# A down projection that takes the gate and up projections' form: two slices of an FFN on one core

## The chip, the cores and the metric

The kernel runs on one core of a Trainium2 chip. The metric is device time in microseconds (us) of that core for one launch. Five engines work side by side, each with its own queue of instructions: PE (matmuls; PEld is the same engine's weight load), DVE (elementwise work), ACT (copies and functions), POOL, and SP, which here mostly issues DMA loads. A matmul holds one operand in the array (the stationary one, 128x128) and streams the other past it; its sums go to PSUM, eight banks of 128 x 512 f32 words. All data are float32. The reference is computed to nearly full float32 precision by splitting each operand into a high part (`hi`, rounded to the type that a PE takes in one pass, F32R) and the remainder (`lo`), and by adding three products: hi*hi, hi*lo and lo*hi.

## The reference

One encoder layer for two request groups that share weights: 256 positions of a new stream and 64 of a running one, together T = 320 columns. The parts ahead of the FFN are left out here; the change touches only the FFN (D = 2048, D_FF = 5632).

```python
h = x + merged @ w_out[l]
hn = rmsnorm(h, norm_ffn[l])
gu = hn @ w_gate_up[l]
h = h + (jax.nn.silu(gu[..., :D_FF]) * gu[..., D_FF:]) @ w_down[l]
...
return rmsnorm(x, norm_final), ...
```

## The kernel before

Activations lie with features on the 128 partitions and the 320 positions on the free axis, so a projection's output block m (128 features x 320 positions) is a sum over the k blocks of its input. D is 16 blocks, D_FF is 44. The FFN runs in three slices of 16, 16 and 12 blocks of D_FF (`SLICES`). For each slice the kernel makes the gate and up projections of these blocks, four blocks at a time, then the down projection of the slice into all 16 blocks of the residual stream `hs`.

There are two forms of a projection:

- **Narrow** (`block`, `product`, lines 84 to 100, and the loop over `lead`, lines 687 to 695). The weight is the stationary operand. For each weight block 128x128 there are three matmuls over 320 columns: high weight with high activation (L87), high weight with low activation (L88), low weight with high activation (L89). `weights` (L75) loads 128x1024 f32 (512 KB) by SP's queue; `halved` (L67) makes the high part on ACT (L70) and the low part on DVE (L71). The result leaves PSUM with one addition on DVE (`down_out`, L671). At the start of a slice's down projection six outputs are built together (`lead`), first from the slice's first eight blocks, so that the last blocks of `act` have time to be finished.
- **Wide** (`quad`, lines 543 to 578). Four output blocks at once, called a quad here. For each k the high weight is now the streamed operand, 512 columns wide (four output blocks of 128), and the activation is stationary, in five pieces: two 128-column pieces of its high part, the two matching pieces of its low part, and one piece that holds the 64 last positions of both. That is the main part of a quad: 16 k x 5 = 80 matmuls (L562) into three PSUM banks, with eight loads of 512 KB (L546), each covering two k. The low weights follow in the narrow form: 4 outputs x 16 k = 64 matmuls of 320 columns (L572), each output's sum copied to `total` by DVE (L573). The main part comes out with positions on partitions, so it has to be turned: `quad_turn` copies the three banks to `flat` as two planes of 16-bit halves on ACT (L587) and issues one DMA transpose per plane from ACT's queue (L588). `quad_join` merges the turned planes on DVE (L594, two copies), adds them to `total` (L596, L597), and `gate_out` (rms factor L601, Silu on ACT L602) or `up_out` (L606, L607, split into hi and lo L610, L611) finishes four blocks. `lows` holds the eight low weight tiles of a quad until the low sums use them: four buffers of tag `wl` and five of tag `low`, nine in turn (`count[0] % 9`). Raw weights have three buffers, high weights four.

What sets the order: every engine takes its instructions in the order of its queue, and that order is the scheduler's, from the order in which the code issues them. `tick()` counts steps (one for each loaded tile, one for each low sum), and `at(tick, fn)` puts work that is due later behind such a step: the join is issued five steps after the main part's end, the two halves of gate_out or up_out at six and seven. PSUM has three banks `acc`, four `aux` and one `aux1`. Gate quads build in `acc`, up quads in `aux`; the low sums take `aux1` and `aux` by turns.

A tile of `act` is hi and lo, 320 columns each. The same pool ("D", 24 buffers) holds the 16 `act` pairs of one slice and the 8 pairs of `hs`.

Of the kernel before, what the change touches and what calls it, by code (L numbers as in the profile page):

```python
# [34 lines left out]
def stream_step(ctx: ExitStack, tc: tile.TileContext, xT, w_in, w_a, w_b, w_out, w_gu, w_down,  # L35
# [501 lines left out]

    fctx = ExitStack()
    fpool = fctx.enter_context(tc.tile_pool(name="ffn", bufs=1))
    count = [0]  # L540

    def quad(b0, main, done):
        lows = []
        for c in range(0, KD, 2):
            raw = wraw.tile([P, HALF * P], F32, tag="raw", name="raw")
            nc.sync.dma_start(out=raw.rearrange("p (b k) -> p b k", b=4),  # L546
                              in_=w_gu[b0 : b0 + 4, :, c * P : (c + 2) * P].rearrange("b p k -> p b k"))
# [6 lines left out]
            nc.scalar.copy(out=wh, in_=raw)  # L554
            nc.vector.tensor_tensor(out=wl, in0=raw, in1=wh.bitcast(F32), op=ALU.subtract)  # L555
            wh = wh.rearrange("p (b k) -> p b k", b=4)
            lows.append(wl)
            for j in range(2):
                k = c + j
                w, x = wh[:, :, j * P : (j + 1) * P], hg[k][2]  # L560
                for i, at0 in enumerate((0, T + TS, P, T + TS + P, TP)):
                    nc.tensor.matmul(main[i // 2].rearrange("p (b m) -> p b m", b=4), x[:, at0 : at0 + P], w,  # L562
                                     start=k == 0 and i % 2 == 0, stop=k == KD - 1 and (i % 2 == 1 or i == 4))
            tick()
        total = fpool.tile([P, 4, T], F32, tag="sum", bufs=2, name="sum")
        now = state["tick"]
        turning = quad_turn(main)
        for b in range(4):
            ps = aux1() if b % 2 == 0 else aux()
            for k in range(KD):  # L570
                at0 = (2 * b + k % 2) * P
                nc.tensor.matmul(ps[:, :T], lows[k // 2][:, at0 : at0 + P], hg[k][0], start=k == 0, stop=k == KD - 1)  # L572
            nc.vector.tensor_copy(total[:, b, :], ps[:, :T])  # L573
            tick()
        at(now + 5, quad_join, total, *turning)
        for i in range(2):
            at(now + 6 + i, done, total, 2 * i)
        return total

    def quad_turn(main):  # L580
# [7 lines left out]
            nc.scalar.dma_start_transpose(out=turned[:, i], in_=planes[:, i, :])  # L588
        return flat, turned

    def quad_join(total, flat, turned):
        rows = flat.bitcast(U16).rearrange("p (b c t w) -> p b c t w", b=4, c=3, w=2)
        for i in range(2):
            nc.vector.tensor_copy(rows[:, :, :, :, 1 - i], turned[:, i].rearrange("p (c b) t -> p b c t", c=3))  # L594
# [9 lines left out]
    def up_out(gate, total, b):  # L604
        t = total[:, b : b + 2, :]
        nc.vector.tensor_tensor(out=t, in0=t, in1=got["rh"][:, None, :].to_broadcast([P, 2, T]), op=ALU.mult)  # L606
        nc.vector.tensor_tensor(out=t, in0=t, in1=gate[:, b : b + 2, :], op=ALU.mult)  # L607
        for j in range(2):
            a = pair("act", dt=F32R)
            nc.scalar.copy(out=a[:, 0, :], in_=t[:, j, :])  # L610
            nc.vector.tensor_tensor(out=a[:, 1, :], in0=t[:, j, :], in1=a[:, 0, :].bitcast(F32), op=ALU.subtract)  # L611
            act.append(a)

    def gain(m, half):
        r = CUTS[half]
# [53 lines left out]

    def down_out(m, ps):  # L670
        nc.vector.tensor_tensor(out=hs[m], in0=ps[:, :T], in1=hs[m], op=ALU.add)  # L671
        if s0 + n < KF:
            return
# [5 lines left out]
        nc.vector.tensor_scalar(out=hs[m], in0=hs[m], scalar1=g_fin[:, m : m + 1], scalar2=None, op0=ALU.mult)  # L679

    for s0, n in SLICES:
        act = []
        for b0 in range(s0, s0 + n, 4):
            gate = quad(b0, [acc() for _ in range(3)], gate_out)
            quad(KF + b0, [aux() for _ in range(3)], lambda total, b, gate=gate: up_out(gate, total, b))
        final = s0 + n == KF
        lead = [acc() for _ in range(3)] + [aux() for _ in range(3)]
        for k0, k1 in ((0, HALF), (HALF, n)):
            for m, ps in enumerate(lead):
                w = weights(w_down[m][:, (s0 + k0) * P : (s0 + k1) * P], k1 - k0)  # L690
                for k in range(k0, k1):
                    product(ps, w, k - k0, (act[k][:, 0, :], act[k][:, 1, :]), k == 0, k == n - 1)
                if k1 == n:
                    down_out(m, ps)
                tick()
        halves = [(t[:, 0, :], t[:, 1, :]) for t in act]
        for m in range(len(lead), KD - LATE if final else KD):
            down_out(m, block(w_down[m][:, s0 * P : (s0 + n) * P], halves))
    fctx.close()
    kept = pool("kept")  # L700
    for m in range(KD - LATE, KD):
# [144 lines left out]
```

## Time and profile before

| | us |
|---|---|
| median of 3 runs | 1693.46 (1691.39 to 1704.93) |
| profiled execution, its own time | 1698.68 |
| its span, first to last instruction | 1696.9 |
| PE busy | 1682.7 |
| DVE busy | 971.8 |
| ACT busy | 734.1 |

The FFN in that execution, by the first matmul of each part:

| part | from | us |
|---|---|---|
| gate and up, slice of 16 (8 quads) | 760.88 | 220.32 |
| down, narrow, 16 x 16 blocks | 981.20 | 112.64 |
| gate and up, slice of 16 (8 quads) | 1093.84 | 224.51 |
| down, narrow, 16 x 16 blocks | 1318.35 | 113.30 |
| gate and up, slice of 12 (6 quads) | 1431.65 | 165.25 |
| down of the last slice, and the end | 1596.90 | 100.00 |

The profiled execution took 1698.68 us, of which 1.8 us lie around the span; it is 5.2 us above the median of the runs shown. Matmuls overlap, so PE counts as busy through almost everything; what a stretch costs is read from the start of its first matmul to the start of the next stretch's first. Equal work in two rows of the second table (the two slices of 16) that takes unequal time shows where PE waited.

### The profile page before, as it was taken

To read this page: it belongs to the slowest core of one execution; us is meant where nothing else is said; L and a number is where in the kernel's file an instruction comes from. 1 tells how busy PE (TensorE), PEld (TensorE's weight loads), DVE (VectorE), ACT (ScalarE), POOL (GpSimd) and SP (SyncE) were. 2 spreads that over 40 slices of the span, in tenths; PEclk is the share of its full clock that TensorE was granted. 3 is DMA by queue.
4 is the path that set the end of the run, shared out by engine and by line. 5 is a ranking of instruction groups with operands and counts; after the bars stand their busy time and mean duration, and the time that the engine had idled before them with its cause. 6 is when DMAs were issued, how large, how long until landed. Compare 5 with 4: busy or idle time off the path is not lost.

```text
span 1696.9 us, 25604 instructions
## 1 busy us (share of the span) xinstructions
PE 1682.7 (99%) x10496; PEld 1607.0 (95%) x10496; DVE 971.8 (57%) x1261; ACT 734.1 (43%) x956; POOL 38.9 (2%) x68
## 2 busy tenths in 40 slices
PE   9999999999999999999999999999999999999998
PEld 9999999999999999998988899988888999889898
DVE  7665656544444445556666664446666644475666
ACT  7555645433333333444444532343445323444343
POOL 1100001000000000000000000000000000000000
PEclk9999999999999999999999999999999999999999
DMA  7866555444444444556656655566666545566554
GB/s 280 258 178 177 160 163 164 118 152 151 151 149 149 150 149 162 173 167 178 175 173 182 193 167 150 156 166 170 180 167 189 166 150 162 164 189 174 149 156 124
DMA packets 236982, 285.49 MB, mean 168 GB/s; under 512 B 98081, under 2 KB 194337, under 8 KB 236865
## 3 DMA queue, kind: packets, MB, share of 16 engines
q1 hardware_dynamic: 164016, 257.72, 48.6%
q10 hardware_dynamic: 70224, 17.88, 6.0%
q0 software_dynamic: 2624, 8.26, 1.6%
q8 instruction: 82, 1.34, 0.3%
q14 instruction: 36, 0.29, 0.1%
HBM read 256.03 MB, written 5.51 MB: 154 GB/s over the span
## 4 chain that ended last, share of the span: by engine, by line
PE 87%; DMA 5%; DVE 4%; ACT 2%; issue 1%; ACTq 0%; SPq 0%; DVEq 0%
PE acc L89 18%; PE acc L87 18%; PE acc L88 18%; PE acc L562 9%; PE aux L572 8%; PE aux L562 7%; DMA raw<-w_gu 2%; DMA turned<-flat 2%; PE aux L89 2%; PE aux L88 2%; PE aux L87 2%; ACT flat L587 1%; DVE low L555 1%; DVE flat L594 1%; PE acc L639 1%
## 5 line engine op out<-in xcount | busy, mean ns | idle before, releaser
L70 ACT CAST wh<-raw 128x1024 fp32r<-128x1024 f32 (+2 forms) x296 | 302.7, 1023 | 561.1 <-PE acc L88 382.4
L71 DVE TENSOR_TENSOR wl<-raw,wh 128x1024 fp32r<-128x1024 f32 (+2 forms) x296 | 351.7, 1191 | 224.4 <-ACT wh L70 223.3
L87 PE MATMUL acc<-A,wh 128*128 128x320 f32 x1088 | 337.7, 311 | 0.4 <-ACT A L108 0.4
L88 PE MATMUL acc<-A,wh 128*128 128x320 f32 x1088 | 336.5, 309 | 0.0
L89 PE MATMUL acc<-A,wl 128*128 128x320 f32 x1088 | 336.3, 309 | 0.0
L554 ACT CAST wh<-raw 128x1024 fp32r<-128x1024 f32 x176 | 185.3, 1054 | 317.8 <-DMA raw<-w_gu 259.9
L87 PEld LDWEIGHTS acc<-A,wh 128*128 128x128 f32 x1088 | 204.4, 188 | 2.3 <-issue 1.5
L88 PEld LDWEIGHTS acc<-A,wh 128*128 128x128 f32 x1088 | 204.5, 188 | 0.3 <-DVE A L110 0.3
L89 PEld LDWEIGHTS acc<-A,wl 128*128 128x128 f32 x1088 | 204.3, 188 | 0.2 <-DVE wl L71 0.2
L562 PE MATMUL acc<-wh,A 128*128 128x512 f32 x880 | 203.2, 390 | 1.1 <-ACT wh L554 1.0
L562 PE MATMUL aux<-wh,A 128*128 128x512 f32 x880 | 201.5, 389 | 0.0
L562 PEld LDWEIGHTS acc<-wh,A 128*128 128x128 f32 x880 | 164.2, 188 | 37.0 <-ACT wh L554 3.5
L562 PEld LDWEIGHTS aux<-wh,A 128*128 128x128 f32 x880 | 164.8, 188 | 33.7
L89 PE MATMUL acc<-act,wl 128*128 128x320 f32 x500 | 155.1, 311 | 2.8 <-DVE wl L71 2.8
L87 PE MATMUL acc<-act,wh 128*128 128x320 f32 x500 | 155.0, 310 | 0.0
L88 PE MATMUL acc<-act,wh 128*128 128x320 f32 x500 | 154.9, 310 | 0.0
L555 DVE TENSOR_TENSOR low<-raw,wh 128x1024 fp32r<-128x1024 f32 x96 | 117.8, 1235 | 37.4 <-ACT wh L554 37.1
L573 DVE COPY sum<-aux 128x320 f32<-128x320 f32 x88 | 43.0, 489 | 157.8 <-PE aux L572 157.8
L572 PE MATMUL aux<-A,low 128*128 128x320 f32 x768 | 128.6, 309 | 0.1
L572 PEld LDWEIGHTS aux<-A,low 128*128 128x128 f32 x768 | 117.1, 188 | 1.4 <-ACT flat L587 0.4
L555 DVE TENSOR_TENSOR wl<-raw,wh 128x1024 fp32r<-128x1024 f32 x80 | 97.6, 1224 | 22.1 <-ACT wh L554 22.1
L572 PE MATMUL aux<-A,wl 128*128 128x320 f32 x640 | 109.0, 309 | 0.8 <-ACT flat L587 0.8
(221 smaller groups left out, 2297.5 us busy)
## 6 DMA issues: line engine op xcount, KB each, us to landing
raw<-w_gu SPq DMA_DIRECT2D x176, 512.0 KB, 3.8
raw<-w_in SPq DMA_DIRECT2D x141, 512.0 KB, 3.7
raw<-w_down SPq DMA_DIRECT2D x80, 512.0 KB, 3.7
raw<-w_out SPq DMA_DIRECT2D x32, 512.0 KB, 3.6
raw<-w_a SPq DMA_DIRECT2D x16, 512.0 KB, 3.4
raw<-w_b SPq DMA_DIRECT2D x16, 512.0 KB, 3.5
raw<-w_down SPq DMA_DIRECT2D x16, 256.0 KB, 2.8
xr<-xT POOLq DMA_DIRECT2D x16, 160.0 KB, 2.6
```

Source lines behind the costliest of these rows:

```text
L70: nc.scalar.copy(out=wh[:, : n * P], in_=raw[:, : n * P])
L71: nc.vector.tensor_tensor(out=wl[:, : n * P], in0=raw[:, : n * P], in1=wh[:, : n * P].bitcast(F32), op=ALU.subtract)
L87: nc.tensor.matmul(ps[:, :T], a, x[0], start=first, stop=False)
L88: nc.tensor.matmul(ps[:, :T], a, x[1], start=False, stop=False)
L89: nc.tensor.matmul(ps[:, :T], b, x[0], start=False, stop=last)
L554: nc.scalar.copy(out=wh, in_=raw)
L555: nc.vector.tensor_tensor(out=wl, in0=raw, in1=wh.bitcast(F32), op=ALU.subtract)
L562: nc.tensor.matmul(main[i // 2].rearrange("p (b m) -> p b m", b=4), x[:, at0 : at0 + P], w, start=k == 0 and i % 2 == 0, stop=k == KD - 1 ...
L572: nc.tensor.matmul(ps[:, :T], lows[k // 2][:, at0 : at0 + P], hg[k][0], start=k == 0, stop=k == KD - 1)
L573: nc.vector.tensor_copy(total[:, b, :], ps[:, :T])
L587: tc.keep_in_program_order(nc.scalar.copy(out=planes[:, i, c * 512 : (c + 1) * 512], in_=hw[:, :, 1 - i]))
L594: nc.vector.tensor_copy(rows[:, :, :, :, 1 - i], turned[:, i].rearrange("p (c b) t -> p b c t", c=3))
```

## The change

Four things change, all in the FFN.

1. `quad` takes any source of weights and any list of stationary activations. The down projections of the first two slices (not the last) are made as four quads each, with the slice's 16 `act` blocks as the stationary operands and `w_down` as the streamed one. The result is added to `hs` by `add_down`, four blocks per quad in two additions of 128x640. For this, `up_out` stores the low part of `act` in the piecewise order that the wide form needs (`apart`): two subtractions, 64 and 256 columns, for one of 320.
2. Between a slice's last up quad and its down quads, the first gate quad of the next slice is run; its result waits in a tile of its own (`held`) until the down quads are done.
3. `quad_join` is placed behind the copy of the last low sum (`tc.issue_after(copied.ins)`), and its step and those of the finishing work are each one later (6, 7 and 8).
4. The low weights' ring has eight buffers, four `wl` and four `low`, for nine; PSUM sets `acc` and `aux` alternate by a count of quads.

The last slice's down projection stays narrow, with `lead` outside the loop.

```diff
-    def quad(b0, main, done):
+    def quad(src, xs, done, tag="sum"):
         lows = []
-        for c in range(0, KD, 2):
+        nk = len(xs)
+        main = [(acc, aux)[count[1] % 2]() for _ in range(3)]
+        count[1] += 1
+        for c in range(0, nk, 2):
...
-            if count[0] % 9 < 4:
+            if count[0] % 8 < 4:
                 wl = wsplit.tile([P, HALF * P], F32R, tag="wl", name="wl")
             else:
-                wl = fpool.tile([P, HALF * P], F32R, tag="low", bufs=5, name="low")
+                wl = fpool.tile([P, HALF * P], F32R, tag="low", bufs=4, name="low")
...
-            nc.vector.tensor_copy(total[:, b, :], ps[:, :T])
+            copied = nc.vector.tensor_copy(total[:, b, :], ps[:, :T])
             tick()
-        at(now + 5, quad_join, total, *turning)
+        at(now + 6, quad_join, copied.ins, total, *turning)
         for i in range(2):
-            at(now + 6 + i, done, total, 2 * i)
+            at(now + 7 + i, done, total, 2 * i)
         return total
...
-    def quad_join(total, flat, turned):
+    def quad_join(behind, total, flat, turned):
+        with tc.issue_after(behind):
+            join(total, flat, turned)
...
+            for r0, r1, at0 in (((TP, T, T), (0, TP, T + TS)) if apart else ((0, T, T),)):
+                nc.vector.tensor_tensor(out=flat[:, at0 : at0 + r1 - r0], in0=t[:, j, r0:r1],
+                                        in1=a[:, 0, r0:r1].bitcast(F32), op=ALU.subtract)
+            to.append(a)
+
+    def add_down(m0, total, b):
+        y = ypair[(m0 + b) // 2]
+        nc.vector.tensor_tensor(out=y, in0=total[:, b : b + 2, :], in1=y, op=ALU.add)
...
+        for b0 in range(s0, s0 + n, 4):
+            gate = gate_quad(b0) if held is None else held
+            held = None
+            up_quad(b0, gate, act, not final)
+        if not final:
+            held = gate_quad(s0 + n, "held")
+            wide_act = [t.rearrange("p i t -> p (i t)") for t in act]
+            for m in range(0, KD, 4):
+                quad(w_down[m : m + 4, :, s0 * P : (s0 + n) * P], wide_act, lambda total, b, m=m: add_down(m, total, b))
```

How the instructions stand now, at three places. First PE at the end of the first slice's up quads. Before, the last low sums (L572) are followed by the narrow triples of the down projection, 768 matmuls of 320 columns:

```order
L572 MATMUL aux<-A,wl 128x320 x4
L572 MATMUL aux<-A,low 128x320 x10
L572 MATMUL aux<-A,wl 128x320 x2
L87 MATMUL acc<-act,wh 128x320
L88 MATMUL acc<-act,wh 128x320
L89 MATMUL acc<-act,wl 128x320
L87 MATMUL acc<-act,wh 128x320
L88 MATMUL acc<-act,wh 128x320
```

Now, at the same place (`acc<-wh,A` is the held gate quad, `<-wh,act` and `<-act,wl` or `low` the first down quad, and L565 and L575 are what L562 and L572 were):

```order
L575 MATMUL aux<-A,low 128x320 x8
L565 MATMUL acc<-wh,A 128x512 x80
L575 MATMUL aux_9671<-A,wl 128x320 x8
L575 MATMUL aux_9671<-A,low 128x320 x8
L575 MATMUL aux<-A,wl 128x320 x8
L575 MATMUL aux<-A,low 128x320 x8
L575 MATMUL aux_9707<-A,wl 128x320 x8
L575 MATMUL aux_9707<-A,low 128x320 x8
L575 MATMUL aux<-A,wl 128x320 x8
L575 MATMUL aux<-A,low 128x320 x8
L565 MATMUL aux<-wh,act 128x512 x80
L575 MATMUL aux_9893<-act,wl 128x320 x8
```

What moved: a gate quad stands between the last up quad and the down projection, and each four outputs of the down projection are 80 matmuls of 512 columns and 64 of 320, where they were 192 of 320.

Second, DVE around the join of an up quad (the first of the FFN). L573 copies the low sums, L594 merges the turned planes, L555 makes low weights, of this quad's last tiles (`x4`) and then of the next quad's. Before:

```order
L555 TENSOR_TENSOR low<-raw,wh 128x1024 x4
L573 COPY sum<-aux_8053 128x320
L573 COPY sum<-aux 128x320
L573 COPY sum<-aux_8089 128x320
L555 TENSOR_TENSOR low<-raw,wh 128x1024
L594 COPY flat<-turned 128x1536
L573 COPY sum<-aux 128x320
L594 COPY flat<-turned 128x1536
L555 TENSOR_TENSOR wl<-raw,wh 128x1024
```

Now (L576, L601 and L558 are the same instructions):

```order
L558 TENSOR_TENSOR low<-raw,wh 128x1024 x3
L576 COPY sum<-aux_8053 128x320
L576 COPY sum<-aux 128x320
L576 COPY sum<-aux_8089 128x320
L558 TENSOR_TENSOR wl<-raw,wh 128x1024 x2
L576 COPY sum<-aux 128x320
L601 COPY flat<-turned 128x1536 x2
L558 TENSOR_TENSOR wl<-raw,wh 128x1024
```

What moved: the last low sum's copy now stands ahead of the first merging copy, and one more of the next quad's low weights is made between the third and the fourth low sum (it was the last of the `x4` before). In both, two low weights of the next quad stand ahead of the join and the third behind it.

Third, DVE at the end of the last up quad, where the last slice's narrow down projection begins (L71 makes that projection's low weights). Before, both merging copies stand ahead of its first low weight:

```order
L573 COPY sum<-aux 128x320
L594 COPY flat<-turned 128x1536
L573 COPY sum<-aux_14633 128x320
L594 COPY flat<-turned 128x1536
L71 TENSOR_TENSOR wl<-raw,wh 128x1024
L573 COPY sum<-aux 128x320
L71 TENSOR_TENSOR wl<-raw,wh 128x1024
```

Now two of these low weights stand ahead of the join:

```order
L576 COPY sum<-aux 128x320
L576 COPY sum<-aux_14441 128x320
L71 TENSOR_TENSOR wl<-raw,wh 128x1024 x2
L576 COPY sum<-aux 128x320
L601 COPY flat<-turned 128x1536 x2
L71 TENSOR_TENSOR wl<-raw,wh 128x1024
```

What moved: the join, from ahead of the third low sum's copy to behind the fourth's, and with it the first two low weights of the down projection, which no longer stand behind it.

More of the change, by code (lines that the diff above doesn't have):

```diff
@@ L559, in quad @@
                 k = c + j
[L560 removed]
+                w, x = wh[:, :, j * P : (j + 1) * P], xs[k]
                 for i, at0 in enumerate((0, T + TS, P, T + TS + P, TP)):
                     nc.tensor.matmul(main[i // 2].rearrange("p (b m) -> p b m", b=4), x[:, at0 : at0 + P], w,
[L563 removed]
+                                     start=k == 0 and i % 2 == 0, stop=k == nk - 1 and (i % 2 == 1 or i == 4))
             tick()
[L565 removed]
+        total = fpool.tile([P, 4, T], F32, tag=tag, bufs=2 if tag == "sum" else 1, name=tag)
         now = state["tick"]
@@ L589, in quad_turn, with join @@
         return flat, turned
-    def quad_join(total, flat, turned):
+    def quad_join(behind, total, flat, turned):
+        with tc.issue_after(behind):
+            join(total, flat, turned)
+    def join(total, flat, turned):
         rows = flat.bitcast(U16).rearrange("p (b c t w) -> p b c t w", b=4, c=3, w=2)
@@ L602, in gate_out, with up_out @@
         nc.scalar.activation(out=t, in_=t, func=AF.Silu)
-    def up_out(gate, total, b):
+    def up_out(to, apart, gate, total, b):
         t = total[:, b : b + 2, :]
@@ L671, in down_out @@
         nc.vector.tensor_tensor(out=hs[m], in0=ps[:, :T], in1=hs[m], op=ALU.add)
-        if s0 + n < KF:
-            return
         if m == 0:
@@ L679, in down_out, with gate_quad, up_quad @@
         nc.vector.tensor_scalar(out=hs[m], in0=hs[m], scalar1=g_fin[:, m : m + 1], scalar2=None, op0=ALU.mult)
+    wide_x = [t[2] for t in hg]
+    def gate_quad(b0, tag="sum"):
+        return quad(w_gu[b0 : b0 + 4], wide_x, gate_out, tag)
+    def up_quad(b0, gate, to, apart):
+        quad(w_gu[KF + b0 : KF + b0 + 4], wide_x, lambda total, b: up_out(to, apart, gate, total, b))
+    held = None
     for s0, n in SLICES:
         act = []
+        final = s0 + n == KF
         for b0 in range(s0, s0 + n, 4):
-            gate = quad(b0, [acc() for _ in range(3)], gate_out)
@@ L685, in stream_step @@
[L685 to L695, printed above, removed]
@@ L696, in stream_step @@
-        halves = [(t[:, 0, :], t[:, 1, :]) for t in act]
-        for m in range(len(lead), KD - LATE if final else KD):
-            down_out(m, block(w_down[m][:, s0 * P : (s0 + n) * P], halves))
+            gate = gate_quad(b0) if held is None else held
+            held = None
+            up_quad(b0, gate, act, not final)
[4 more added lines that the diff above has]
+                quad(w_down[m : m + 4, :, s0 * P : (s0 + n) * P], wide_act, lambda total, b, m=m: add_down(m, total, b))
@@ new lines, in stream_step @@
+    lead = [acc() for _ in range(3)] + [aux() for _ in range(3)]
+    for k0, k1 in ((0, HALF), (HALF, n)):
+        for m, ps in enumerate(lead):
+            w = weights(w_down[m][:, (s0 + k0) * P : (s0 + k1) * P], k1 - k0)
+            for k in range(k0, k1):
+                product(ps, w, k - k0, (act[k][:, 0, :], act[k][:, 1, :]), k == 0, k == n - 1)
+            if k1 == n:
+                down_out(m, ps)
+            tick()
+    halves = [(t[:, 0, :], t[:, 1, :]) for t in act]
+    for m in range(len(lead), KD - LATE):
+        down_out(m, block(w_down[m][:, s0 * P : (s0 + n) * P], halves))
```

11 lines of the change are left out of this document (5 added, 6 removed).

## The prediction

> **What bounds the kernel now.** I read the page first, then the stretches of the FFN, then PE in order of time at each place where a stretch is longer than its matmuls, and then the engine that PE waited for there.
>
> ```profile
> span 1696.9 us, 25604 instructions
> PE 1682.7 (99%) x10496; PEld 1607.0 (95%) x10496; DVE 971.8 (57%) x1261; ACT 734.1 (43%) x956; POOL 38.9 (2%) x68
> PE 87%; DMA 5%; DVE 4%; ACT 2%; issue 1%; ACTq 0%; SPq 0%; DVEq 0%
> ```
>
> PE is busy 99% of the span and carries 87% of the chain that ended last; DVE and ACT have room. So the change is worth what it takes off PE: a shorter stream of matmuls, and fewer gaps in it. The stretches of the FFN (columns: window, length, busy time of PE, PEld, DVE, ACT, POOL, clock, DMA share, GB/s):
>
> ```profile
> 760.88:981.20 220.32, 220.32 (x1155) 195.20 (x1154) 137.05 (x162) 105.27 (x138) 2.15 (x1) 1.00 0.65 179
> 981.20:1093.84 112.64, 112.64 (x771) 112.64 (x770) 55.99 (x61) 33.95 (x35) 0.00 (x0) 1.00 0.51 155
> 1093.84:1318.35 224.51, 222.50 (x1155) 194.72 (x1153) 133.74 (x155) 101.78 (x133) 0.00 (x0) 1.00 0.64 174
> 1318.35:1431.65 113.30, 112.89 (x770) 112.63 (x769) 55.84 (x61) 33.95 (x35) 0.00 (x0) 1.00 0.51 157
> 1431.65:1596.90 165.25, 165.25 (x866) 146.41 (x865) 95.06 (x111) 75.00 (x98) 0.00 (x0) 1.00 0.62 175
> ```
>
> The first down projection is 768 narrow matmuls in 112.64 us: 146.7 ns each. The first slice's eight quads take 220.32, 27.54 each, and the last slice's six 165.25, again 27.54: no gap. The second slice lost 224.51 - 220.32 = 4.19 us in its quads and 113.30 - 112.64 = 0.66 in its down projection. One quad on PE:
>
> ```profile
> 1139.57 1.33 PE L572 MATMUL aux<-A,wl 128*128 128x320 f32 x8
> 1148.95 18.32 PE L562 MATMUL acc<-wh,A 128*128 128x512 f32 x80
> 1167.11 0.45 PE L572 MATMUL aux<-A,low 128*128 128x320 f32 x2
> ```
>
> From 1148.95 to 1167.11 are 18.16 us for 80 matmuls of 512 columns, 227.0 ns each; the low sums ahead of them took 9.38, that is 64 at 146.6.
>
> **Part 1, the down projection of two slices in the wide form.** For four outputs, 192 narrow matmuls are replaced by 80 + 64: 28.16 us by 27.54. A slice of 16 has four such quads, 110.16 for 112.64, and two slices save 2 x 2.48 = 4.96 us. The columns streamed are the same (61,440 per four outputs in both forms); what is saved is the cost of 48 matmuls that no longer exist. A stretch of w_down with act as the stationary operand isn't in this trace. The nearest row is the gate quad's, of the same shape, 227.0 ns. The other end is the narrow row's price per column, 146.7 x 512 / 320 = 234.7 ns, at which nothing is saved. I take 227.0, since 1,760 such matmuls ran at it.
>
> The Trainium skill, "TensorE: Matmul & The Clock Gate", Back-to-back issue gap, has a matmul at N / 2.4 + 2.5 ns, so 215.8 and 135.8 here. The rows show 227.0 and 146.7, about 13.5 ns over the streaming and not 2.5, and the measurement decides; by the page's figures I estimate a saving of 0.96 us where the rows give 4.96.
>
> What the quads add off PE, from these groups:
>
> ```profile
> L587 ACT COPY flat<-acc 128x512 uint16<-128x512 uint16 x66 | 34.3, 592 | 7.6 <-ACT wh L554 6.6 <-PE acc L562 1.1
> L588 ACTq DMA_TRANSPOSE turned<-flat x44: 1430/1450/1692, 780.1 to 1593.1; - x44
> L594 DVE COPY flat<-turned 128x1536 uint16<-128x1536 uint16 x44 | 45.3, 1051 | 40.6 <-DMA turned<-flat 40.6
> L606 DVE TENSOR_TENSOR sum<-sum,rh 128x640 f32<-128x640 f32 x22 | 17.1, 822 | 0.0
> raw<-w_gu SPq DMA_DIRECT2D x176, 512.0 KB, 3.8
> raw<-w_down SPq DMA_DIRECT2D x80, 512.0 KB, 3.7
> ```
>
> ACT gets six plane copies and two transposes per quad, 6 x 0.59 + 2 x 1.45 = 6.5 us, 26 per slice beside the 33.95 it was busy. DVE gets two merges of 1.05 and, at L606's price, two additions into hs of 0.82, besides sums and copies that quads of gate and up have too; those quads keep DVE busy 137.05 / 8 = 17 us and ACT 13 of 27.54. That is the cover, about 10 us each per quad; if it were gone PE would show gaps in all quads of the first slice, and it shows none. The split of act's low part makes 32 more DVE instructions, at most 0.5 us each, in quads with that same cover (0.49 is the 128x320 copy's price in part 3; these are 64 and 256 wide). SP issues as many loads (64 of 512 KB); cut as w_gu's they land in 3.8 us for 3.7. Nothing new is on POOL.
>
> **Part 2, the held gate quad.** It only changes places: its eight loads are ahead of the down projection's 32 on SP's queue, and act now has 27.54 us of PE work to be finished under. I cost it at nothing: finishing a quad is part of DVE's 17 us per quad, so it ends inside the next one. The second slice's 0.66 us (narrow triples waiting for a low weight behind a late join) goes with the narrow form.
>
> **Part 3, the join behind the fourth low sum.** A quiet quad (DVE, then ACT's casts for the next quad's last loads):
>
> ```profile
> 1147.22 1.22 DVE L555 TENSOR_TENSOR wl<-raw,wh 128x1024 fp32r<-128x1024 f32 x1
> 1150.21 1.06 DVE L594 COPY flat<-turned 128x1536 uint16<-128x1536 uint16 x1 [1.78 <-DMA turned<-flat]
> 1151.14 0.49 DVE L573 COPY sum<-aux 128x320 f32<-128x320 f32 x1
> 1152.47 1.23 DVE L555 TENSOR_TENSOR wl<-raw,wh 128x1024 fp32r<-128x1024 f32 x1
> 1162.38 1.05 ACT L554 CAST wh<-raw 128x1024 fp32r<-128x1024 f32 x1
> ```
>
> What stands behind the join on DVE is the next quad's third low weight; only then is a raw buffer free, SP loads, ACT casts, PE streams. The join began 1150.21 - 1139.57 = 10.64 us after the low sums did; the last cast ended at 1163.43 and PE needed it after 70 matmuls, 1148.95 + 70 x 0.227 = 1164.84. The slack is 1.4 us. In a late quad:
>
> ```profile
> 1208.43 1.07 DVE L594 COPY flat<-turned 128x1536 uint16<-128x1536 uint16 x1 [4.58 <-DMA turned<-flat]
> 1204.42 11.52 PE L562 MATMUL acc<-wh,A 128*128 128x512 f32 x50
> 1216.55 2.59 PE L562 MATMUL acc<-wh,A 128*128 128x512 f32 x10 [0.61 <-ACT wh L554]
> 1224.34 0.89 PE L572 MATMUL aux<-A,low 128*128 128x320 f32 x5
> 1194.65 0.74 PE L572 MATMUL aux<-A,low 128*128 128x320 f32 x4
> 1315.90 0.56 PE L572 MATMUL aux<-A,wl 128*128 128x320 f32 x2 [0.75 <-ACT flat L587]
> ```
>
> Here it began 13.78 us after, 3.14 later; less the slack, 1.74 us should be lost, and 1224.34 - 1204.42 - 18.16 = 1.76 were. So a quad loses what its join begins after about 12.0. Now two low weights (from 7.65 after the low sums' start, 1.13 apart) and the copy stand ahead: the join can begin at about 10.4 and has no copy between its halves, so it may begin as late as 12.4. The last row is another quad of that slice, where PE itself waited for a PSUM bank that ACT's plane copies had not emptied. Copies and transposes were late where they stood behind casts that waited for loads; with eight buffers the fourth load of the next quad starts at about 8.9 and no longer beside the transposes. So I expect the 4.19 us to be gone. Both ends: all kept (0 gained), or lateness in more quads (a rival below).
>
> **Part 4, the end of the last up quad.**
>
> ```profile
> 1596.83 1.05 DVE L594 COPY flat<-turned 128x1536 uint16<-128x1536 uint16 x1 [3.93 <-DMA turned<-flat]
> 1599.07 1.21 DVE L71 TENSOR_TENSOR wl<-raw,wh 128x1024 fp32r<-128x1024 f32 x1
> 1597.63 0.31 PE L88 MATMUL acc<-act,wh 128*128 128x320 f32 x1
> 1600.33 0.64 PE L89 MATMUL acc<-act,wl 128*128 128x320 f32 x1 [2.39 <-DVE wl L71]
> 1603.52 0.31 PE L89 MATMUL acc<-act,wl 128*128 128x320 f32 x1
> 1600.33:1603.40 3.07, 3.07 (x12) 3.07 (x13) 3.07 (x4) 0.00 (x0) 0.00 (x0) 0.52 0.61 172
> ```
>
> The first low weight of the last down projection stood behind the join; PE stopped, and after the gap the granted clock was 0.52 for 3.07 us. From 1597.63 to 1603.52 are 5.89 us for 13 matmuls worth 1.91: 3.98 us lost. Now two low weights stand ahead of the join, enough for 48 matmuls, 7.0 us, and the first needs no more than 7.65 + 1.2 of the 9.38 us of low sums. The 3.98 us go. Next late is the third, due 16.4 us after the low sums' start and done at about 13.8.
>
> **The sum**, against the profiled execution: 1698.68 - 4.96 - 0.66 - 4.19 - 3.98 = 1684.9. That execution stands 5.2 us above the median of 1693.46, about as much as the second slice's 4.85, which I take for late transposes of that one execution. By the median, without those terms: 1693.46 - 4.96 - 3.98 = 1684.5. Both agree; if the runs of the median have the second slice's gaps as well, 1693.46 - 13.79 = 1679.7.
>
> **The rivals.**
>
> Only the stream is saved: the gaps come back elsewhere (another late low weight at the last slice, other late transposes). 1693.46 - 4.96 = 1688.5. For it: each gap has its own cause in a queue's order, and all orders changed. Against: the new order names no late step.
>
> The fixed cost per matmul is not saved in the new stretch, because act's tiles stream no better than the narrow form: 227.0 becomes up to 234.7, and the forecast becomes 1684.9 + 4.0 to 5.0, about 1689. The page's rule above would give this too. Against: the same shape ran at 227.0 throughout.
>
> Slower: the ring of eight. With the spare buffer gone, the next quad's first low weight can't be made until the fourth low sum has read its tile. If this moves loads so that they run beside the transposes, and the joins of all 30 quads begin later than 12.4 us after the low sums' start, each loses the excess. The forecast's 9 us are eaten at 0.3 us per quad (join at 12.7), and 1% is lost at 0.85 (13.3, while the late quad above had 13.78): at that quad's 13.78, 30 x 1.4 = 42, so 1726. For it: several quads of one slice were late like this. Against: the two low weights that stand ahead of the join are the same in number as before.
>
> **How the numbers follow.** The forecast holds 0.72, its own range 1679 to 1690; only the stream 0.14; no saving per matmul 0.04; the ring of eight 0.10, half of it within 1%. About 1%, 17 us, is what a measurement of this kernel can tell from no change (the three runs lie 13.5 apart). Nothing in the sum reaches 1676.5: faster by over 1% 0.02; slower 0.05; within 1% 0.93. The range goes from 1678 (all gaps in the median, a little more) to 1696 (only the stream, and the mild half of the ring).
>
> **What would show it.** Right: each of the two down stretches takes 110.2 us from first 512-wide matmul to the next up quad's; 30 quads of 27.54; no PE gap at the last down projection and a clock of 1.00 there; DVE's first merge of a quad begins 10.4 to 12 us after the low sums. Wrong: PE gaps ended by ACT's casts at a quad's sixth to eighth load, main parts over 18.16, or matmuls over 227 ns.

## The result and the profile after

| | median us | runs |
|---|---|---|
| before | 1694.11 | 20, 1691.27 to 1714.24 |
| after | 1710.47 | 20, 1699.85 to 1719.59 |

The ratio is 1.0079, 95% interval 1.0055 to 1.0103: slower by 0.8%, 25.6 us above the forecast of 1684.9 and outside its range. Medians and ratios, here and below, leave out a run marked as slow (over 1.5% above the fastest of the same kernel); that is one of e9's four. The profiled execution took 1711.4 us, with a span of 1709.6. From the page of the changed kernel, the span, the engines, and the chain of work that ended last:

```profile
span 1709.6 us, 24995 instructions
PE 1684.1 (99%) x10112; PEld 1575.8 (92%) x10112; DVE 1008.9 (59%) x1341; ACT 759.7 (44%) x1004; POOL 38.9 (2%) x68
PE 75%; DMA 11%; DVE 6%; ACT 4%; issue 2%; ACTq 1%; SPq 0%; DVEq 0%
```

The busy share of PE says nothing here: it is 99% in both kernels. What moved is the chain: PE carries 75% of it for 87%, DMA 11% for 5%, DVE and ACT 10% for 6%. The stretches, with the columns of the prediction's (nine quads, four down quads, eight quads, four down quads, five quads, the end):

```profile
760.57:1010.47 249.90, 248.75 (x1299) 219.36 (x1297) 156.31 (x202) 117.53 (x155) 2.15 (x1) 1.00 0.65 176
1010.47:1122.76 112.29, 110.80 (x578) 97.45 (x577) 65.08 (x73) 47.09 (x58) 0.00 (x0) 1.00 0.62 175
1122.76:1353.46 230.70, 224.15 (x1154) 194.26 (x1153) 143.19 (x185) 101.06 (x134) 0.00 (x0) 1.00 0.65 175
1353.46:1467.21 113.75, 111.87 (x579) 97.14 (x578) 65.23 (x73) 47.10 (x58) 0.00 (x0) 1.00 0.62 173
1467.21:1613.61 146.40, 141.07 (x722) 123.85 (x721) 86.93 (x103) 62.77 (x82) 0.00 (x0) 0.98 0.63 172
1613.61:1709.62 96.01, 88.10 (x602) 87.52 (x600) 67.27 (x135) 39.19 (x71) 0.00 (x0) 0.98 0.49 145
```

At 27.54 us a quad the first five rows should be 247.86, 110.16, 220.32, 110.16 and 137.70. They are 2.04, 2.13, 10.38, 3.59 and 8.70 longer: 26.84 us lost in the 30 quads. The end took 96.01 where it took 100.00. The account closes: 1684.9 + 26.84 = 1711.7, for the 1711.4 measured. So the other terms of the sum came out, and the quads, whose 4.19 us of gaps were to go, lost 26.84 instead.

**The worst quad.** Its low sums began at 1457.82. First ACT, from the last cast ahead of the plane copies, then DVE, then PE in the next quad's main part:

```profile
1461.38 1.05 ACT L557 CAST wh<-raw 128x1024 fp32r<-128x1024 f32 x1 [1.64 <-DMA raw<-w_gu]
1462.33 1.55 ACT L590 COPY flat<-acc 128x512 uint16<-128x512 uint16 x3
1463.91 1.46 ACTq L591 DMA_TRANSPOSE turned<-flat  x1
1465.41 1.56 ACT L590 COPY flat<-acc 128x512 uint16<-128x512 uint16 x3 [1.53 <-issue]
1467.01 1.64 ACTq L591 DMA_TRANSPOSE turned<-flat  x1
...
1465.47 2.35 DVE L558 TENSOR_TENSOR wl<-raw,wh 128x1024 fp32r<-128x1024 f32 x2
1467.74 0.48 DVE L576 COPY sum<-aux 128x320 f32<-128x320 f32 x1
1476.43 1.97 DVE L601 COPY flat<-turned 128x1536 uint16<-128x1536 uint16 x2 [8.21 <-DMA turned<-flat]
1478.28 1.21 DVE L558 TENSOR_TENSOR wl<-raw,wh 128x1024 fp32r<-128x1024 f32 x1
...
1467.21 9.25 PE L565 MATMUL aux<-wh,A 128*128 128x512 f32 x40
1477.34 2.56 PE L565 MATMUL aux<-wh,A 128*128 128x512 f32 x10 [0.88 <-ACT wh L557]
1484.35 9.89 PE L565 MATMUL aux<-wh,A 128*128 128x512 f32 x30 [4.45 <-ACT wh L557]
```

Read it from the top. The plane copies waited on ACT behind a cast that waited for a load of the next quad. So the second transpose was issued 9.2 us after the low sums' start, and the join, ready on DVE at 1468.2, waited 8.21 us for it. The third low weight stood behind the join, with it the load that its raw buffer lets go, and PE ran out of high weights twice. This main part took 26.86 us for 18.16. In the second gap PE stood for 4.45 us, and the granted clock behind it was 0.50:

```profile
1484.35:1490.20 5.85, 5.85 (x14) 4.59 (x15) 3.92 (x4) 2.10 (x2) 0.00 (x0) 0.50 0.81 244
```

What the transpose met, by the DMA view of 1462 to 1478 (tile, issues, KB, median us from issue to landing; the 6.3 is the median of 3.7 and 8.95):

```profile
raw<-w_gu SPq DMA_DIRECT2D x2, 512.0 KB, 6.2
turned<-flat ACTq DMA_TRANSPOSE x2, 6.3
```

The two low weights that stand ahead of the join let two raw buffers go. Their loads were issued at 1466.7 and 1467.8 and landed after 4.17 and 8.30 us; the second transpose, issued between them, took 8.95. Over all transposes, before and then after:

```profile
DMA to landing us min/median/max: 3.6/3.7/6.1
...
DMA to landing us min/median/max: 3.6/3.8/9.0
```

Sorted by its own issue, the second transpose of a quad in the changed kernel landed after 3.83 us on the mean where it was issued less than 7.5 us after the low sums' start (21 quads), and after 6.19 us where later (9 quads, 7.8 to 9.6 us). Those nine are the nine whose join began later than 12.4 us.

### The profile page after: what moved, and what is told of

The parts are those of the page before. It is cut to its first block, busy times and chain, and to the rows that moved or that the text cites. A ratio compares the mean times of both kernels' runs of the same rounds, so it can differ in the third digit from the quotient of the medians.

```text
span 1709.6 us, 24995 instructions
## 1 busy us (share of the span) xinstructions
PE 1684.1 (99%) x10112; PEld 1575.8 (92%) x10112; DVE 1008.9 (59%) x1341; ACT 759.7 (44%) x1004; POOL 38.9 (2%) x68
## 4 chain that ended last, share of the span: by engine, by line
PE 75%; DMA 11%; DVE 6%; ACT 4%; issue 2%; ACTq 1%; SPq 0%; DVEq 0%
PE acc L87 14%; PE acc L88 14%; PE acc L89 14%; PE aux L575 9%; PE acc L565 9%; PE aux L565 8%; DMA turned<-flat 4%; DMA raw<-w_down 4%; DMA raw<-w_gu 3%; ACT flat L590 2%; DVE low L558 2%; ACT wh L557 2%; DVE flat L601 2%; ACTq L591 1%; DVE sum L603 1%
## 5 line engine op out<-in xcount | busy, mean ns | idle before, releaser
L557 ACT CAST wh<-raw 128x1024 fp32r<-128x1024 f32 x240 | 252.6, 1053 | 436.3 <-DMA raw<-w_gu 282.2
L70 ACT CAST wh<-raw 128x1024 fp32r<-128x1024 f32 (+2 forms) x232 | 235.7, 1016 | 406.0 <-PE acc L88 290.8
L71 DVE TENSOR_TENSOR wl<-raw,wh 128x1024 fp32r<-128x1024 f32 (+2 forms) x232 | 273.4, 1182 | 164.4 <-ACT wh L70 164.2
L565 PE MATMUL aux<-wh,A 128*128 128x512 f32 x880 | 205.8, 394 | 7.0 <-ACT wh L557 7.0
L565 PE MATMUL acc<-wh,A 128*128 128x512 f32 x880 | 204.8, 391 | 3.8 <-ACT wh L557 3.7
L565 PEld LDWEIGHTS aux<-wh,A 128*128 128x128 f32 x880 | 166.4, 190 | 43.4 <-ACT wh L557 9.1
L565 PEld LDWEIGHTS acc<-wh,A 128*128 128x128 f32 x880 | 163.8, 188 | 41.7 <-ACT wh L557 8.6
L576 DVE COPY sum<-aux 128x320 f32<-128x320 f32 x112 | 54.8, 489 | 234.9 <-PE aux L575 234.9
L558 DVE TENSOR_TENSOR low<-raw,wh 128x1024 fp32r<-128x1024 f32 x120 | 147.2, 1234 | 40.1 <-ACT wh L557 39.9
L558 DVE TENSOR_TENSOR wl<-raw,wh 128x1024 fp32r<-128x1024 f32 x120 | 143.9, 1219 | 7.1 <-PE aux L575 3.7
L575 PE MATMUL aux<-A,wl 128*128 128x320 f32 x704 | 117.6, 309 | 2.2 <-ACT flat L590 2.2
L575 PE MATMUL aux<-A,low 128*128 128x320 f32 x704 | 117.5, 309 | 0.0
L575 PEld LDWEIGHTS aux<-A,wl 128*128 128x128 f32 x704 | 107.6, 188 | 4.4 <-ACT flat L590 2.7
L575 PEld LDWEIGHTS aux<-A,low 128*128 128x128 f32 x704 | 106.9, 188 | 0.0
L601 DVE COPY flat<-turned 128x1536 uint16<-128x1536 uint16 x60 | 59.4, 1045 | 42.5 <-DMA turned<-flat 40.8
L87 PE MATMUL acc<-mh,wh 128*128 128x320 f32 x256 | 79.1, 309 | 0.0
```

The source lines that it names most:

```text
L70: nc.scalar.copy(out=wh[:, : n * P], in_=raw[:, : n * P])
L71: nc.vector.tensor_tensor(out=wl[:, : n * P], in0=raw[:, : n * P], in1=wh[:, : n * P].bitcast(F32), op=ALU.subtract)
L87: nc.tensor.matmul(ps[:, :T], a, x[0], start=first, stop=False)
L576: copied = nc.vector.tensor_copy(total[:, b, :], ps[:, :T])
```

## The experiments

Two questions: what makes the transposes late, and what makes a late one slow. A quad's turn is its plane copies and its two transposes. "Ring" is the number of low weight buffers. Lost in the quads is, as above, the time over 27.54 per quad in the profiled execution; transposes and joins are counted from the start of their quad's low sums.

**e1: the changed kernel with nine buffers.** Room for the ninth comes from two kinds of scratch tile (`bb` and `xr`) that share another's place.

```diff
-        refine(r, ms, t320("bb"))
+        refine(r, ms, t320("mg", 1))
...
-        x = t320("xr")
+        x = t320(f"gate{m % 2}", 1)
...
-            if count[0] % 8 < 4:
+            if count[0] % 9 < 4:
...
-                wl = fpool.tile([P, HALF * P], F32R, tag="low", bufs=4, name="low")
+                wl = fpool.tile([P, HALF * P], F32R, tag="low", bufs=5, name="low")
```

> The changed kernel with nine low-weight buffers again (room for the ninth is made by sharing three scratch tiles ahead of the FFN). Theory RING (the lost spare buffer makes two loads of every quad start together at 8.9 and 10.0 us after the low sums' start, where they fall on the second transpose): the loss of about 27 us in the 30 quads mostly goes, 1685 to 1692 us, ratio to the kernel before 0.995 to 0.999. Theory TURN (the transposes are issued late because plane copies stand on ACT behind casts that wait for loads): little changes, 1700 to 1711, since the casts stand where they did. Theory JOIN (the join's new place): 1705 to 1711.

1685.78 us (7 runs, 1685.37 to 1686.80), ratio to before 0.9892 (0.9855 to 0.9928). The page's chain and three stretches, the four first down quads, the four later ones, and all 30 quads:

```profile
PE 99%; DVE 0%; DMA 0%; SPq 0%; ACT 0%; issue 0%; DVEq 0%
...
1008.52:1118.68 110.16, 110.16 (x578) 97.60 (x577) 64.75 (x73) 46.99 (x58) 0.00 (x0) 1.00 0.66 182
1339.00:1449.16 110.16, 110.16 (x578) 97.60 (x577) 64.65 (x73) 46.76 (x58) 0.00 (x0) 1.00 0.66 182
...
760.65:1586.86 826.21, 826.21 (x4322) 731.98 (x4321) 514.51 (x632) 373.75 (x487) 2.15 (x1) 1.00 0.66 180
```

The last row is 30 x 27.54 = 826.2: nothing is lost. The quad that was the worst above, here with its low sums from 1439.78:

```profile
1439.58 1.05 ACT L557 CAST wh<-raw 128x1024 fp32r<-128x1024 f32 x1 [1.43 <-DMA raw<-w_gu]
1440.54 1.54 ACT L590 COPY flat<-acc 128x512 uint16<-128x512 uint16 x3
1442.03 1.05 ACT L557 CAST wh<-raw 128x1024 fp32r<-128x1024 f32 x1
1442.11 1.47 ACTq L591 DMA_TRANSPOSE turned<-flat  x1
1443.62 1.56 ACT L590 COPY flat<-acc 128x512 uint16<-128x512 uint16 x3 [0.54 <-ACT wh L557]
1445.21 1.45 ACTq L591 DMA_TRANSPOSE turned<-flat  x1
...
1450.39 1.97 DVE L601 COPY flat<-turned 128x1536 uint16<-128x1536 uint16 x2
```

The same cast ended 0.85 us after the low sums' start, not 4.6, the second transpose was issued at 5.4, and the join found its data there at 10.6. This is what the ninth buffer does. With it, one low weight of the next quad can be made before the low sums begin, so a raw buffer is free, and the loads and casts of the next quad come a step earlier. With eight, that low weight has to wait until the low sums release a tile, some 7.6 us after they begin, and ACT's casts wait for loads just when the plane copies are due behind them.

e1's time fits its theory RING, but the mechanism named there does not hold: with nine buffers, too, two loads start at 8.9 and 10.0 us in every quad (the next quad's fifth and sixth, where with eight they are the fourth and fifth). What differs is the transposes: in e1 the second transpose of each quad was issued at 4.2 to 6.0 us, and no join began after 10.9. That is TURN's mechanism, and TURN's own time for e1 (1700 to 1711) was a miss, since the casts did not stand where they did.

**e3: eight buffers, but the plane copies don't wait.** The casts of the next quad's first three tiles are placed behind the second transpose on ACT.

```diff
+    last = [None]
...
-            nc.scalar.copy(out=wh, in_=raw)
+            if last[0] is None or c > 4:
+                nc.scalar.copy(out=wh, in_=raw)
+            else:
+                with tc.issue_after(last[0]):
+                    nc.scalar.copy(out=wh, in_=raw)
...
+            sent = nc.scalar.dma_start_transpose(out=turned[:, i], in_=planes[:, i, :])
+        last[0] = sent.ins
```

> The changed kernel with the first three casts of a quad placed on ACT's queue behind the previous quad's second transpose, so that plane copies wait for PE alone. TURN: second transposes are issued about 4.3 us after the low sums' start in every quad, land before 8.9 in about 3.7 us each, joins begin at 10.3, quads take 27.54, and the time is 1683 to 1688, ratio 0.994 to 0.997. RING alone: the two loads still start at 8.9 and 10.0, so if these hurt by themselves (late for PE, not by meeting a transpose) the loss stays, over 1700. JOIN: the loss stays, 1705 to 1711.

1685.86 us (9 runs, 1685.01 to 1687.45), ratio 0.9924 (0.9896 to 0.9952); 0.04 us lost in the quads, as TURN expected. ACT in the quad that was the worst, and all 30 quads:

```profile
1440.21 1.56 ACT L595 COPY flat<-acc 128x512 uint16<-128x512 uint16 x3 [3.62 <-PE acc L570]
...
1444.90 1.45 ACTq L596 DMA_TRANSPOSE turned<-flat  x1
...
761.53:1587.77 826.24, 826.24 (x4322) 732.00 (x4321) 515.28 (x632) 373.28 (x487) 2.15 (x1) 1.00 0.66 180
```

The plane copies now wait for PE alone. The second transpose goes out at 4.2 to 5.1 us in every quad but the last (6.8), and the two loads still start at 8.9 and 10.0. So with the join at its new place eight buffers cost nothing by themselves: they cost what the casts ahead of the plane copies wait. The shared scratch tiles aren't what e1 gained by: e3 has none of them, and e9 below has them and is slow.

**e4: the kernel before with e3's edit.**

> The kernel before with the same edit. TURN: its second slice's gaps, where a run has them, go; the gap at the last down projection shrinks or stays, since the join still stands ahead of that low weight: 1687 to 1693, ratio 0.996 to 1.000. RING and JOIN: no change, 1692 to 1697.

1702.80 us (10 runs, 1700.82 to 1703.70), ratio 1.0027 (1.0001 to 1.0053): a miss. The quads still lost 5.72, and the end got worse. DVE and PE at the last down projection:

```profile
1601.49 1.02 DVE L600 COPY flat<-turned 128x1536 uint16<-128x1536 uint16 x1 [4.39 <-DMA turned<-flat]
1602.40 1.22 DVE L71 TENSOR_TENSOR wl<-raw,wh 128x1024 fp32r<-128x1024 f32 x1
...
1603.67 0.41 PE L89 MATMUL acc<-act,wl 128*128 128x320 f32 x1 [3.56 <-DVE wl L71]
```

The edit covers the casts in `quad`, not those of `weights` (L70), which stand ahead of the last quad's plane copies; and the join at its old place still has the narrow projection's first low weight behind it. Of the second transposes only those of each slice's last quad were issued after 7.5 us (8.3 to 9.7). The gap at the last down projection was 3.56 us, for 2.39 before. An early turn doesn't replace the join's new place.

**e6: the kernel before with the join's new place alone** (nine buffers, narrow down projection).

```diff
-        at(now + 5, quad_join, total, *turning)
+        at(now + 6, behind, copied.ins, total, *turning)
...
+    def behind(ins, total, flat, turned):
+        with tc.issue_after(ins):
+            quad_join(total, flat, turned)
```

> The kernel before (narrow down projections, nine low-weight buffers) with only the join placed behind the fourth low sum's copy and its steps one later. Theory TERMS (the sum of the prediction holds where no transpose is late): the 3.98 us gap at the last down projection goes, and the second slice's gaps with it or not: 1687 to 1691, ratio 0.996 to 0.998. Theory JOIN (the join's new place costs time by itself): 1695 or more.

1690.24 us (10 runs, 1689.90 to 1690.99), ratio 0.9952 (0.9927 to 0.9976); 0.03 us lost in the quads. The chain, and the FFN up to the last down projection:

```profile
PE 99%; DMA 0%; DVE 0%; SPq 0%; ACT 0%; issue 0%; DVEq 0%
...
761.06:1592.25 831.19, 831.19 (x4707) 762.06 (x4706) 478.13 (x551) 349.32 (x439) 2.15 (x1) 1.00 0.62 172
```

Against e1's 826.21 this prices the wide form: 4.98 us for two slices. The times differ by 4.46. The theory TERMS held.

**e2, e9, e5, e10: the other combinations.** e2 is the kernel before with `% 8` and four `low`; e9 is e1 with the join at its old place; e5 is the changed kernel with the join at its old place; e10 is e6 with eight buffers.

> The kernel before with eight low-weight buffers and nothing else changed. RING: its 22 quads lose about 0.9 us each as in the changed kernel, 20 us, so 1708 to 1716, ratio 1.008 to 1.013. TURN: some loss only, 1694 to 1702. JOIN: no change, 1692 to 1697.

> The changed kernel with nine low-weight buffers and the join where it was before (no order behind the copy, steps 5 to 7). TERMS: against nine buffers with the new join (1685.8), the gap of about 4 us at the last down projection comes back and the quads have less slack: 1689 to 1697. If the join's place is worth nothing: 1685 to 1687.

> The kernel after (eight buffers, wide down quads) with the join at its old place. Two theories of what the join's new place does when the ring has eight buffers. RING: the loss comes from the eight buffers, and the new place softens it. The kernel before with eight buffers and the old place lost 35.84 us in 22 quads, 1.63 each; 30 quads at that price lose 49, so 1685.8 + 49 = 1735, and anything above 1722 speaks for it. PLACE: with eight buffers it is the new place itself that makes the joins late (two low weights and a copy stand ahead of it). Then the old place loses less than the changed kernel's 26.85, and the time is 1710 or less.

> The kernel before (narrow down projection) with eight buffers and the join at its new place; the nine-buffer version of it took 1690.24. RING: eight buffers alone make turns late in any quad: at the changed kernel's 26.85 / 30 = 0.9 us per quad, 22 quads lose 20, so about 1710; 1696 to 1714 speaks for it. WIDE: the wide down quads carry the lateness on, since they follow each other without a stretch in which ACT can catch up (in the changed kernel the first eleven quads lost 2.4 of the 26.85). Then the two narrow stretches end each chain of late quads and less than 5 us are lost: 1690 to 1695.

| down projection | ring | join | median us | ratio to before | lost in quads, us |
|---|---|---|---|---|---|
| narrow | 9 | old (before) | 1694.11 | 1 | 4.2 |
| narrow | 9 | new (e6) | 1690.24 | 0.9927 to 0.9976 | 0.03 |
| narrow | 8 | old (e2) | 1731.48 | 1.0104 to 1.0231 | 35.8 |
| narrow | 8 | new (e10) | 1697.06 | 0.9954 to 1.0008 | 1.6 |
| wide | 9 | old (e9) | 1728.85 | 1.0048 to 1.0229 | 42.5 |
| wide | 9 | new (e1) | 1685.78 | 0.9855 to 0.9928 | 0.02 |
| wide | 8 | old (e5) | 1732.64 | 1.0179 to 1.0243 | 42.4 |
| wide | 8 | new (after) | 1710.47 | 1.0055 to 1.0103 | 26.8 |

Each ratio is to runs of the kernel before that were taken beside it; their medians went from 1694.1 to 1699.3, so a difference of medians between two rows can be off by some 5 us. By the medians, the eight buffers cost 37 us with the old place and the narrow form, 6.8 with the new place (by the ratios 0.3%, 4.9 us), and 24.7 with the new place and the wide form.

e2 is a miss for all three of its theories, which ended at 1716. e9 is a miss: nine buffers don't carry the wide form with the join at its old place. Its first eleven quads lost 0.04 us together, and from the third down quad on every turn was late, 19 of 30 second transposes issued after 7.5 us; what starts this there stays open.

e10 fits neither of its theories alone: its median is at the low end of what was to speak for RING (from 1696), its profiled execution, 1693.78 us with 1.6 lost, in the range of WIDE. What speaks for the theory that wide quads carry lateness on: in e10, at the first quad behind each narrow stretch, the next quad's first cast starts 6.6 us ahead of the low sums; in the changed kernel, at the first quad behind each four down quads, it starts 1.2 and 3.2 us ahead, much as in its other quads (median 2.1). No run tested that by itself.

e5's time fits RING (above 1722) and not PLACE. But few of its transposes were late (3 of 30), and yet it lost 42.4. DVE and PE show another wait:

```profile
872.27 1.22 DVE L558 TENSOR_TENSOR wl<-raw,wh 128x1024 fp32r<-128x1024 f32 x1
876.08 1.05 DVE L601 COPY flat<-turned 128x1536 uint16<-128x1536 uint16 x1 [2.60 <-DMA turned<-flat]
...
878.34 1.21 DVE L558 TENSOR_TENSOR wl<-raw,wh 128x1024 fp32r<-128x1024 f32 x1
...
884.37 5.13 PE L565 MATMUL acc<-wh,A 128*128 128x512 f32 x20 [1.10 <-ACT wh L557]
```

Here one low weight stands ahead of the join, not two. With eight buffers it is the next quad's first, so the second one, and the fifth load behind it, wait for the join even when that begins at 11.45 us. PE, at the fifth tile (after 40 matmuls), waits. The second low weight stands behind the join in 19 of the 29 quads of e5 that another quad follows (in the other ten it stands ahead). In these 19 the next quad's fifth load starts at 14.3 us (median), not at 10.0, and the quads that follow them lost 41.8 of the 42.4 us. In e2 it is 11 of 19 quads, followed by 35.3 of the 35.8 us. So at the old place the loss with eight buffers comes where this order stands on DVE.

**e7 and e8: is a late transpose slow, or only late?** e7 makes the turn late: e3's edit for the third cast alone, and six idle ACT copies of 128x320 ahead of the second plane. e8 is e7 with the next quad's first two low weights placed behind the join, so that no load starts while the transposes run. The idle copies write a scratch tile that nothing reads any more.

```diff
+            for _ in range(6 if i else 0):
+                scratch = t320("gate0", 1)
+                tc.keep_in_program_order(nc.scalar.copy(out=scratch, in_=hg[0][0].bitcast(F32)))
...
+            if last[0] is not None and c < 4:
+                at(state["tick"] + 2 - c // 2, lower)
```

> Eight buffers, transposes ahead of the third cast, and six idle copies of 128x320 on ACT (work that adds nothing to the output) ahead of each quad's second plane, so that the second transpose is issued about 3 us later, at about 7.5 us after the low sums' start, with two loads starting at 8.9 and 10.0. Theory COLLISION (a second transpose still in flight when the two loads start takes 5 us and more from issue to landing for 3.7): median of 5 us or more, joins at 12.5 to 14, and a loss of 0.5 to 2 us in most of the 30 quads, 1700 to 1740. Theory LATE ONLY (a transpose takes 3.7 us whenever it is issued): joins at about 11.3, no loss, 1685 to 1688.

> As the kernel with the late second transpose, but the first two low weights of the next quad stand behind the join on DVE, so that none of its fourth and fifth loads can start before both transposes have landed. The kernel must get slower for another reason (PE then waits for those loads in every quad, 1750 to 1900); what is asked is the second transpose's time from issue to landing. COLLISION: about 3.7 us although it is issued as late. LATE ONLY or another cause on ACT's side: the same as in the kernel with the late second transpose, whatever that is.

e7 took 1776.37 us, beyond the 1700 to 1740 of COLLISION (its second transposes went out at 7.0 to 11.9 us, not at about 7.5), and e8 1847.08 (one run each; what counts here is the transposes). From issue to landing, e7 and then e8:

```profile
DMA to landing us min/median/max: 3.6/4.3/9.9
...
DMA to landing us min/median/max: 3.6/3.7/12.2
```

In e7, 26 second transposes were issued 7.5 us or more after the low sums' start and took 6.67 us on the mean; the four issued earlier took 3.80. In e8, PE runs some of a quad's low sums inside its main part, so its transposes are counted from the main part's last matmul on. Second transposes went out 7.1 to 9.6 us after it, 23 of them at 7.5 or more; these 23 landed within 3.70 us, and 29 of 30 within 4.11. The thirtieth is the last quad's, where loads of the narrow down projection, which the edit doesn't hold back, started beside it. The DMA view of one of the 29, and of the thirtieth:

```profile
turned<-flat ACTq DMA_TRANSPOSE x1, 3.7
...
raw<-w_down SPq DMA_DIRECT2D x3, 512.0 KB, 10.2
turned<-flat ACTq DMA_TRANSPOSE x1, 12.2
```

So it is the loads beside it that make a transpose slow, and not its lateness.

The Trainium skill, "DMA: Bandwidth & Descriptors", Queues, rings and completion order, says that each DMA engine takes packets from its queues by turns. The rows agree with that as far as they go: transposes and loads that run together are slow together (8.95 beside 4.17 and 8.30; 12.2 beside a median of 10.2), where alone both take 3.7.

## Why the prediction was wrong

**Part 1 was right.** Four wide down quads take 110.16 us, as worked out, in e1; e6 against e1 gives 4.98 for the term of 4.96. The work on ACT and DVE costs PE nothing in e1, so its cover was there. The formula of the Trainium skill ("TensorE: Matmul & The Clock Gate", Back-to-back issue gap), from which 0.96 was estimated, is given there for a single, isolated matmul and not for a stream of weight loads and matmuls like this one; the prediction used it for such a stream, and was right to go by its rows.

**Part 2 was right.** The gate and up quads, the two held ones among them, lose nothing in e1 and e3 (all 30 quads together 0.02 and 0.04), and the 0.66 us is gone.

**Part 3 failed.** It priced the eight buffers at nothing, in one sentence: with eight buffers the fourth load starts at about 8.9 "and no longer beside the transposes". The load does start at 8.9, and another at 10.0. So do two loads in e1, where nothing is lost. What sets the transposes' issue is ACT's queue. The prediction saw that they are late behind casts that wait for loads, but did not work out where eight buffers put those casts: the buffer that is gone takes one early low weight with it, the next quad's loads and casts slide back behind it, the plane copies stand behind those casts, and the second transpose goes out at 7.8 to 9.6 in nine quads, where e1 has 4.2 to 6.0. There it runs into just those two loads. The term of 4.19 was to be gone; 26.84 came in its place: 22.7 in the main parts, where PE waited for high weights, and 4.1 in the low sums of three quads, where it waited for a PSUM bank that the plane copies had not emptied (the wait of the last row in part 3). What part 3 says of a late join's price is borne out: the nine joins began 22.1 us later than 12.4, taken together. e1 (loads early again) and e3 (copies no longer behind casts) each take all of it away.

That 1693.46 already lay low for lack of late transposes fits, but is not shown, since one execution of the kernel before was profiled: e6, without late transposes, has runs within 1.1 us of each other, while the kernel before spreads over 23.

**Part 4 was right**: 3.99 us for 3.98. The last quad of the changed kernel on DVE, and the clock in the first 7 us of the last down projection:

```profile
1611.88 2.35 DVE L71 TENSOR_TENSOR wl<-raw,wh 128x1024 fp32r<-128x1024 f32 x2
1614.14 0.48 DVE L576 COPY sum<-aux 128x320 f32<-128x320 f32 x1
1615.30 1.99 DVE L601 COPY flat<-turned 128x1536 uint16<-128x1536 uint16 x2 [0.68 <-DMA turned<-flat]
...
1613.61:1620.61 7.00, 7.00 (x50) 7.00 (x49) 6.32 (x7) 2.10 (x2) 0.00 (x0) 1.00 0.73 213
```

Two low weights are ready before the join; PE has no gap and keeps its clock.

**The sum and the rivals.** Without the late turns the sum holds: 1684.9 against 1685.78 (e1) and 1685.86 (e3). The rival of the ring of eight came true, by the mechanism that it named, loads beside the transposes, but not in its form. It supposed that all 30 joins slide by the same amount; nine of 30 were late, by 0.7 to 6.2 us, and the mean price was 26.84 / 30 = 0.89 us per quad. Its chance of 0.10 was too small for a change that takes a buffer out of the one loop whose lateness the profile already showed (six of the 22 second transposes of the kernel before were issued after 7.5 us). The argument against it counted the low weights ahead of the join, and not those ahead of the low sums.

**The sign that was to show it wrong** was the one that came: PE gaps ended by ACT's casts, and main parts over 18.16 us.

## What to carry to other kernels

When a change takes a buffer out of a ring, follow what that buffer let run early, through every engine's queue, up to the transfer that it starts; don't stop at the engine that fills it. A short wait of an engine off the critical path (here 1.6 us of ACT) can push a transfer into the time of others, and the collision costs more than the wait. Here either repair is small, nine buffers or the plane copies ahead of the casts, and both beat the kernel before: 1685.8 against 1694 to 1699.

## What the runs showed of the hardware

A DMA transpose of one plane landed about 3.65 us after its issue when no load started beside it (29 second transposes of e8: 3.65 to 4.11). It took 5.1 to 9.0 us in the nine late ones of the changed kernel, up to 9.9 in e7 and once 12.2 in e8, when loads of 512 KB started beside it; those loads were slower too, up to 8.3 and 10.2 us for 3.7. A stop of PE of 4.45 us was followed by a granted clock of 0.50 for the next 5.85 us, in which 14 matmuls ran that are worth 3.18.
